# Gate and up projections of layer 0's second half: twelve slices as seven block products

## The chip, the cores and the metric

The kernel runs on one core of a Trainium2 chip. The metric is the device time of one execution in microseconds. Times in this document are medians of several runs, or come from one profiled execution where they are split into parts.

## The reference, cut to what matters

The model is a decoder trunk of two layers that computes one inference step for a prompt of 1024 tokens and a sample group of 8 tokens with the same weights. Each layer mixes the tokens (a gated recurrence in layer 0, stick-breaking attention in layer 1, in both beside attention into a memory) and then applies a SwiGLU feed-forward network. The change is in that network alone:

```python
def swiglu(h, w_gu, w_down):
    gate, up = jnp.split(h @ w_gu, 2, axis=-1)
    return (jax.nn.silu(gate) * up) @ w_down

h = h + rmsnorm(swiglu(rmsnorm(h, g[2]), w_gu[l], w_down[l]), g[3])
```

`h` has 1024 channels, `gate` and `up` 2816 each. Everything is in float32.

## The kernel before

**Groups and halves.** The tokens are worked on in two groups: group 0 has 512 prompt tokens, group 1 the other 512 and the 8 sample tokens, 520 columns in two halves of 260. Activations stand transposed: channels on the partitions, tokens along the columns. "The first half" of a layer is group 0's way through it, "the second half" group 1's.

**One projection.** To keep float32 accuracy every operand is split into a rounded part and the rest (`split_to` L280, `split_w` L250): ACT casts, DVE subtracts. A product takes three matmuls for each 128 x 128 block of weights: high by high, high by low, low by high. `proj` (L266) computes 128 output channels: it loads the weights in blocks of 512 x 128 over SP's queue into `wraw` (5 buffers), splits them into `wspl` (5 buffers), and accumulates eight blocks of 128 input channels in a tile of two PSUM banks, `mmp`, of which there are 2. For group 1 each matmul covers one half, 260 columns, so one projection is 8 x 3 x 2 = 48 matmuls.

**The feed-forward network.** The 2816 channels are 22 slices of 128, in five parts (`PARTS`, L613): 5, 5, 4, 4 and 4 slices. In `ffn.part` (L693) a slice is one projection for gate, SiLU by exponential, logarithm and exponential (`silu`, L284), one projection for up, the product of both, and its split into a tile of `mpool`. After the slices of a part comes the part's share of the down projection: eight products over the part's 4 or 5 slices, added into the result by `evac_raw` (L441).

**The seven products.** The last layer's second half (`ffn_w`, L615) already takes another way for its slices from the fifth on. `gate_up_w` (L524) regards gate and up of a slice as a product of 2 x 2 blocks: the weights' rows in two halves of 512, gate and up; the tokens in two halves of 260. By Winograd's form of Strassen's scheme it takes 7 block products of 4 x 3 = 12 matmuls (`product`, L546) where there were 8, 84 matmuls a slice in place of 96. It needs

- four sums of weight blocks, which `weight_sums` (L588) makes in DRAM: for each part eight DMAs of 1 MB (1.25 MB in the longer parts) on POOL's queue, four plain copies and four that accumulate. Each is let go by a mark: ACT copies one column of a tile just made (`after()`) into a small tile `tok`, POOL copies it on, and the DMA is issued behind that.
- four combinations of activations for each of four pairs of channel blocks, which `sums_w` (L326) makes on DVE and splits with ACT;
- four accumulators `pa` to `pd` (L557). They are chained: `pb` begins as the negated copy of `pa`, made by ACT after product 0, and `pc` as the negated copy of `pb` after product 2.

The products' order in a slice is: 0 into `pa`, 1 into `pd`, 2 into `pb`, 3 into `pa`, 4 into `pb`, 5 into `pc`, 6 into `pb`. In the last layer's second half the projections' PSUM tiles have been closed, and each accumulator has two banks of its own. Weight blocks are loaded there into `wraw` and, in every other case, into halves of tiles of `apool`.

**Order of work.** The program is recorded as generators that `weave` (L232) mixes by the weights written beside them; each `yield` is a step. A scheduler then orders the instructions of each engine. Around the change the text reads (L1462 to L1481, shortened):

```python
    f0 = ffn(0, 0, o0.x)
    weave((a1.core(), 22), (f0.part(0), 9))
    a1.open()
    weave((a1.sample(), 6), (a1.gate(), 4), (f0.part(1), 9))
    weave((chain(a1.merge(), a1.mem()), 12), (a1.mem_sample(), 20), (chain(f0.part(2), f0.part(3)), 16))
    drain(f0.part(4))
    ...
    f1 = ffn(1, 0, o1.x)
    ws = weight_sums(1, range(5), lambda: f1.now)
    weave((chain(b0.sb(), b0.mem()), 24), (chain(f1.part(0), f1.part(1)), 18), (islice(ws, 16), 17))
    weave((chain(f1.part(2), f1.part(3), f1.part(4)), 24), (ws, 24))
```

So `f0`, the first half's network of layer 0, runs beside the second group's mixer `a1`, which also reads the sample tokens' memory caches. `f1`, the second half's network of layer 0, runs parts 0 and 1 beside layer 1's mixer of the first group (`b0`) and parts 2 to 4 alone. Beside all of `f1`, layer 1's weight sums are made in DRAM.

Of the kernel before, what the change touches and what calls it, by code (L numbers as in the profile page):

```python
# [9 lines left out]
F32 = mybir.dt.float32  # L10
F32R = mybir.dt.float32r
# [13 lines left out]
def tile_decoder(  # L25
# [61 lines left out]
    def Q(i):  # L87
        return single[0].tile([P, 512], F32, tag=f"q{i}", name=nm("q"))
# [234 lines left out]
            out.append(x)  # L323
            yield

    def sums_w(xs, ops):  # L326

        n, h = NG[1], PW[1]  # L330
        for k in range(4):
            x0, x1 = xs[k], xs[k + 4]
            y = YT()
            if k % 2 == 0:
                z, u = YT(), YT()
            o = (k % 2) * h

            def full(x, c):
                t = B()
                nc.vector.tensor_add(t[:, :h], x[:, 0, c : c + h].bitcast(F32), x[:, 1, c : c + h].bitcast(F32))  # L340
                return t

            b11, b12, b21, b22 = full(x0, 0), full(x0, h), full(x1, 0), full(x1, h)
            for d, p, a, b in (
                (b11, u[:, :, o : o + h], b12, b11), (b12, y[:, :, h : 2 * h], b12, b22),
                (b22, y[:, :, :h], b22, b11), (b21, z[:, :, o : o + h], b21, b22),
            ):
                nc.vector.tensor_sub(d[:, :h], a[:, :h], b[:, :h])
# [7 lines left out]
    def YT():  # L356
        return xpool.tile([P, 2, NG[1]], F32R, tag="x0", name=nm("y"))

    def wo_tiles(g):
# [161 lines left out]
        split_to((mt[:, 0, :n], mt[:, 1, :n]), sg[:, :n])  # L521
        return mt, last

    def gate_up_w(l, f, ops, spl, raws):  # L524

        h, n = PW[1], NG[1]
        part, o = part_of(f)
# [26 lines left out]
                        start=(first and k == 0 and wi == 0), stop=(k == 3 and wi == 2), skip_group_check=True,  # L554
                    )

        pa, pb, pc, pd = (Q(i) for i in range(4))  # L557
        product(pa, 0, True)
        nc.scalar.activation(pb[:, :h], pa[:, :h], AF.Copy, scale=-1.0)
        product(pd, 1, True)  # L560
# [10 lines left out]
        product(pc, 5)  # L571
        nc.vector.tensor_sub(gt[:, :h], pc[:, :h], dt[:, h:n])
        product(pb, 6)
        nc.scalar.activation(sg[:, h:n], gt[:, :h], AF.Silu)
        nc.vector.tensor_mul(sg[:, :h], sg[:, :h], pb[:, :h])
# [3 lines left out]
        return mt  # L579

    sums = {}

# [32 lines left out]
    class ffn_w:  # L615


        def __init__(self, l, x, plain):
            self.g, self.l, self.x, self.ops, self.plain, self.n, self.r, self.pi = 1, l, x, [], plain, 0, 0, 0
            self.R = self.acc = None  # L620
            self.half = []
            self.sums = sums_w(x, self.ops)

        def spl(self):
            self.n += 1
# [13 lines left out]
        def part(self, pi):  # L639
# [4 lines left out]
            for j in range(nf):  # L644
                self.pi = pi
                if f0 + j < self.plain:
                    mt, ins = gate_up_q(l, f0 + j, self.x)
                    mids.append(mt)
                    with tc.issue_after(ins.ins):
                        for _ in range((1, 2, 1, 0)[j]):  # L650
                            next(self.sums, None)
                else:
                    mids.append(gate_up_w(l, f0 + j, self.ops, self.spl, self.raws))
                yield
            if pi == 0:
                self.R = R_one()
# [29 lines left out]
            yield from finish_rows(self)  # L686

    class ffn:
        def __init__(self, g, l, xt, rows=False):
            self.g, self.l, self.xt, self.rows = g, l, xt, rows  # L690
            self.R = self.acc = None

        def part(self, pi):  # L693
            g, l = self.g, self.l
# [2 lines left out]
            last = pi == len(PARTS) - 1  # L697
            mids = []
            for j in range(nf):
                pg = proj(g, w_gu[l], 0, ND, (f0 + j) * P, self.xt)  # L700
                sg = silu(None, pg, g)
                pu = proj(g, w_gu[l], 0, ND, DFF + (f0 + j) * P, self.xt)
                nc.vector.tensor_mul(sv(sg, g), sv(sg, g), pv(pu, g))  # L703
                mt = M(F32R)
                split_to((mt[:, 0, :n], mt[:, 1, :n]), sg[:, :n])
                mids.append(mt)
                self.now = sg[:, 0:1]
                yield
            if pi == 0:
                self.R = R_one()  # L710
            if last:
                self.acc = small([P, WID], tag="st", bufs=3)
            for m in range(ND):
                ps = proj(g, w_down[l], f0, nf, m * P, mids)
                evac_raw(g, self.R, ps, m, self.acc, pi == 0, last)
                self.now = self.R[m][:, 0:1]
                if last and self.rows:
                    nc.scalar.activation(
                        self.R[m][:, :n], self.R[m][:, :n], AF.Copy, scale=gcol(l, 3, m)
                    )  # L720
                    if m == 3:
                        first_half(self)
                if m % 2:
                    yield

        def finish(self, store):
# [733 lines left out]
    drain(o0.mm(a0.xo))  # L1460
    weave((o0.finish(), 17), (chain(a1.v(), a1.qm(A)), 8))
    f0 = ffn(0, 0, o0.x)  # L1462
    weave((a1.core(), 22), (f0.part(0), 9))
    a1.open()
    weave((a1.sample(), 6), (a1.gate(), 4), (f0.part(1), 9))
    weave((chain(a1.merge(), a1.mem()), 12), (a1.mem_sample(), 20), (chain(f0.part(2), f0.part(3)), 16))
    drain(f0.part(4))
    xk0, xb0 = [], []
    o1 = out_proj(1, 0, M)
# [67 lines left out]
```

## Time and profile before

| | us |
|---|---|
| median of 3 runs | 2504.36 (2503.7 to 2506.84) |
| the profiled execution | 2502.81 |
| its span, first to last instruction | 2501.1 |
| TensorE busy in the span | 2468.7 |
| DVE busy | 1571.7 |
| ACT busy | 1185.4 |

The time outside the span is 1.71 us. Layer 0's second half runs its parts 2 to 4 from about 1242 to 1451 us of the span. The views used below are: the page's first part; the timeline of an engine (start, length, engine, line, operation, what it writes and reads, count); a table of stretches with each engine's busy time, the clock that TensorE was granted and the share of the 16 DMA engines; groups of instructions by line (count, busy time and mean duration in ns, then the engine's idle time before them and what ended it); and the DMA view of a stretch, by queue (packets, MB, share) and by issuing line (count, size, median time from issue to landing). q0 is POOL's queue, q1 the one that SP feeds.

### The profile page before, as it was taken

What the parts mean: (1) busy time and instruction counts of PE and PEld (TensorE: products, weight loads), DVE (VectorE), ACT (ScalarE), POOL (GpSimd) and SP (SyncE); (2) the same over time, 40 slices, a digit from 0 to 9 for tenths busy, and PEclk for the clock granted to TensorE, in tenths of its full rate; (3) what the DMA queues carried; (4) which work ended last, traced back from release to release, by engine and by line L of the source; (5) the groups of instructions that cost most, each with busy time, mean ns of one, the idle gap of its engine ahead of it and who ended that gap; (6) DMA issues with size and microseconds to landing.
All of it is one profiled execution on the core that took longest, in us unless ns stands there. A gap on an engine that the chain in (4) does not pass through costs nothing. (4 is left out here: it accounts for less than half of the span.)

```text
span 2501.1 us, 40758 instructions
## 1 busy us (share of the span) xinstructions
PE 2468.7 (99%) x15565; PEld 2169.4 (87%) x15565; DVE 1571.7 (63%) x2756; ACT 1185.4 (47%) x2277; POOL 97.5 (4%) x139
## 2 busy tenths in 40 slices
PE   8999999999999999999999999999999999999998
PEld 6888888877877898999999989877787797999997
DVE  5766556754766585655544475777677648755665
ACT  5446544243434454555433454555444445564444
POOL 1000000000000000010111100022000000000000
PEclk9999999999999999999999999999999999999999
DMA  5352252134543447577678876544354234365542
GB/s 186 114 165 68 69 159 81 54 106 121 180 122 104 128 128 232 162 190 177 168 188 220 230 203 194 160 137 148 118 148 134 80 119 122 121 191 145 150 138 69
DMA packets 496109, 358.21 MB, mean 143 GB/s; under 512 B 19109, under 2 KB 443634, under 8 KB 495914
## 3 DMA queue, kind: packets, MB, share of 16 engines
q1 hardware_dynamic: 477354, 301.08, 40.2%
q0 software_dynamic: 18560, 54.53, 8.8%
q8 instruction: 122, 2.00, 0.3%
q14 instruction: 73, 0.60, 0.1%
HBM read 325.73 MB, written 75.94 MB: 161 GB/s over the span
## 5 line engine op out<-in xcount | busy, mean ns | idle before, releaser
L274 PE MATMUL mm<-x,ws 128*128 128x260 f32 (+1 forms) x7776 | 1344.1, 331 | 0.0
L274 PEld LDWEIGHTS mm<-x,ws 128*128 128x128 f32 x7776 | 1149.9, 188 | 152.9 <-issue 13.1
L260 ACT CAST ws<-w 128x512 fp32r<-128x512 f32 x712 | 420.2, 591 | 750.5 <-PE mm L274 615.1
L261 DVE TENSOR_TENSOR ws<-w,ws 128x512 fp32r<-128x512 f32 x712 | 463.4, 654 | 288.5 <-ACT ws L260 278.1
L274 PE MATMUL mm<-m,ws 128*128 128x512 f32 (+1 forms) x2112 | 400.2, 344 | 0.0
L274 PEld LDWEIGHTS mm<-m,ws 128*128 128x128 f32 x2112 | 324.3, 188 | 48.8 <-issue 2.2
L667 PE MATMUL q<-m,ws 128*128 128x260 f32 x1056 | 128.8, 283 | 0.0
L667 PEld LDWEIGHTS q<-m,ws 128*128 128x128 f32 x1056 | 127.2, 188 | 0.4 <-ACT hT L485 0.2
L543 DVE TENSOR_TENSOR ws<-w,ws 128x512 fp32r<-128x512 f32 x126 | 86.6, 692 | 60.3 <-ACT ws L542 57.6
L552 PE MATMUL q<-y,ws 128*128 128x260 f32 x864 | 112.9, 283 | 0.0
L542 ACT CAST ws<-w 128x512 fp32r<-128x512 f32 x126 | 78.0, 621 | 68.6 <-PE q L667 27.4
L552 PEld LDWEIGHTS q<-y,ws 128*128 128x128 f32 x864 | 107.6, 188 | 0.0
L447 DVE TENSOR_TENSOR r<-r,mm 128x512 f32<-128x512 f32 (+1 forms) x96 | 66.1, 689 | 65.7 <-PE mm L274 64.7
L291 DVE TENSOR_SCALAR t<-mm 128x512 f32<-128x512 f32 (+1 forms) x82 | 56.8, 693 | 78.7 <-PE mm L274 78.4
L703 DVE TENSOR_TENSOR t<-t,mm 128x512 f32<-128x512 f32 (+1 forms) x66 | 45.5, 690 | 75.7 <-PE mm L274 75.2
L295 DVE TENSOR_TENSOR t<-t,t 128x512 f32<-128x512 f32 (+1 forms) x66 | 45.8, 694 | 70.7 <-ACT t L294 70.7
L552 PE MATMUL q<-x,ws 128*128 128x260 f32 x648 | 86.3, 282 | 0.0
L552 PEld LDWEIGHTS q<-x,ws 128*128 128x128 f32 x648 | 81.3, 188 | 0.0
L314 DVE TENSOR_TENSOR st<-st,n 128x512 f32<-128x512 f32 (+1 forms) x98 | 67.3, 694 | 6.9 <-ACT n L313 5.2
L281 ACT CAST m<-t 128x512 fp32r<-128x512 f32 (+1 forms) x88 | 54.9, 624 | 18.4 <-DVE t L703 8.8
L282 DVE TENSOR_TENSOR m<-t,m 128x512 fp32r<-128x512 f32 (+1 forms) x88 | 61.0, 694 | 2.5 <-ACT m L281 1.4
L962 POOL DMA_INDIRECT c<-in_cache_sb_k,pidx x16 | 16.4, 1023 | 1172.9 <-ACT m L445 962.4
(339 smaller groups left out, 2565.6 us busy)
## 6 DMA issues: line engine op xcount, KB each, us to landing
w<-in_w_gu SPq DMA_DIRECT2D x334, 256.0 KB, 3.2
w<-in_w_down SPq DMA_DIRECT2D x160, 256.0 KB, 3.2
w<-in_w_in_a SPq DMA_DIRECT2D x80, 256.0 KB, 3.0
wsum<-in_w_gu POOLq DMA_DIRECT2D x18, 1024.0 KB, 9.0
w<-wsum SPq DMA_DIRECT2D x72, 256.0 KB, 3.7
w<-in_w_o SPq DMA_DIRECT2D x64, 256.0 KB, 2.8
wsum<-in_w_gu POOLq DMA_DIRECT2D x12, 1280.0 KB, 10.6
w<-in_w_mem_kv SPq DMA_DIRECT2D x32, 256.0 KB, 3.0
```

The lines of the kernel that those rows point to most:

```text
L260: nc.scalar.copy(ws[:, 0, :n, :], raw[:, :n, :])
L261: nc.vector.tensor_sub(ws[:, 1, :n, :], raw[:, :n, :], ws[:, 0, :n, :].bitcast(F32))
L274: nc.tensor.matmul(ps[:, a, : PW[g]], wt, xt[k][:, xi, o : o + PW[g]], start=(k == 0 and wi == 0), stop=(k == nk - 1 and wi == 2),)
L281: nc.scalar.copy(dst[0], src)
L282: nc.vector.tensor_sub(dst[1], src, dst[0].bitcast(F32))
L291: nc.vector.tensor_scalar(sv(x, g), pv(ps, g), -44.0, None, op0=ALU.max)
L314: nc.vector.tensor_add(acc[:, :n], acc[:, :n], t[:, :n])
L447: nc.vector.tensor_add(dst, dst, pv(ps, g))
L542: nc.scalar.copy(w[:, 0, :], src)
L543: nc.vector.tensor_sub(w[:, 1, :], src, w[:, 0, :].bitcast(F32))
L552: nc.tensor.matmul(ps[:, :h], w[:, wj, k * P : (k + 1) * P], x[:, xi, :], start=(first and k == 0 and wi == 0), stop=(k == 3 and wi == 2), ...
L667: nc.tensor.matmul(pp[a][:, :h], wt, mids[k][:, xi, a * h : (a + 1) * h], start=(k == 0 and wi == 0), stop=(k == nf - 1 and wi == 2),)
```

## The change

In layer 0's second half the slices 10 to 21, which are parts 2, 3 and 4, are computed by `gate_up_w`. `ffn` takes a parameter `prod`, the first slice that is done so; all other uses keep the old way.

- The four accumulators are the two PSUM tiles of the projections, `ta` (for `pa` and `pd`) and `tb` (for `pb` and `pc`); both buffers of `mmp` are in use by one slice.
- Weight blocks are loaded into `wraw` alone. Of every eight splits three go to `cpool` and five to `wspl`.
- The combinations of activations are made in the second half of part 1's down projection, one call of `sums_w` after every second of its eight products, in the eight buffers of `apool`.
- Layer 0's weight sums of parts 2 to 4, 24 DMAs of 1 MB on POOL's queue, are made beside `f0` in the first half.
- SiLU in these slices is ACT's own function, which needs another activation table; the table of logarithm and exponential is loaded again after the last slice.

```diff
-    def sums_w(xs, ops):
+    def sums_w(xs, ops, YT):
...
-    def gate_up_w(l, f, ops, spl, raws):
+    def gate_up_w(l, f, ops, spl, raws, quads):
...
-        pa, pb, pc, pd = (Q(i) for i in range(4))
+        pa, pb, pc, pd = quads()
...
     class ffn:
-        def __init__(self, g, l, xt, rows=False):
-            self.g, self.l, self.xt, self.rows = g, l, xt, rows
+        def __init__(self, g, l, xt, rows=False, prod=NF):
+            self.g, self.l, self.xt, self.rows, self.prod = g, l, xt, rows, prod
             self.R = self.acc = None
+            self.ops, self.n = [], 0
+            self.sums = sums_w(xt, self.ops, lambda: A(F32R))
+
+        def spl(self):
+            self.n += 1
+            if self.n % 8 in (1, 4, 6):
+                return cpool.tile([P, 2, 512], F32R, tag="c", name=nm("ws"))
+            return wspl.tile([P, 2, 512], F32R, tag="ws", name=nm("ws"))
+
+        def quads(self):
+            ta, tb = (mmp.tile([P, 2, 512], F32, tag="mm", name=nm("mm")) for _ in range(2))
+            return ta[:, 0, :], tb[:, 0, :], tb[:, 1, :], ta[:, 1, :]
...
             for j in range(nf):
+                if f0 + j >= self.prod:
+                    mt, gate = gate_up_w(
+                        l, f0 + j, self.ops, self.spl,
+                        lambda: wraw.tile([P, 4, P], F32, tag="w", name=nm("w")), self.quads,
+                    )
+                    mids.append(mt)
+                    self.now = mt[:, 0, 0:1].bitcast(F32)
+                    yield
+                    continue
                 pg = proj(g, w_gu[l], 0, ND, (f0 + j) * P, self.xt)
...
+            if last and self.prod < NF:
+                with tc.issue_after(gate.ins):
+                    nc.scalar.preload_act_table_set("natural_log_exp_and_others")
...
                 if m % 2:
+                    if f0 + nf == self.prod < NF:
+                        next(self.sums, None)
                     yield
...
     f0 = ffn(0, 0, o0.x)
-    weave((a1.core(), 22), (f0.part(0), 9))
+    ws = weight_sums(0, (2, 3, 4), lambda: f0.now)
+    weave((a1.core(), 22), (f0.part(0), 9), (islice(ws, 8), 8))
     a1.open()
-    weave((a1.sample(), 6), (a1.gate(), 4), (f0.part(1), 9))
-    weave((chain(a1.merge(), a1.mem()), 12), (a1.mem_sample(), 20), (chain(f0.part(2), f0.part(3)), 16))
+    weave((a1.sample(), 6), (a1.gate(), 4), (f0.part(1), 9), (islice(ws, 8), 8))
+    weave((chain(a1.merge(), a1.mem()), 12), (a1.mem_sample(), 20), (chain(f0.part(2), f0.part(3)), 16), (ws, 10))
...
-    f1 = ffn(1, 0, o1.x)
+    f1 = ffn(1, 0, o1.x, prod=10)
```

More of the change, by code (lines that the diff above doesn't have):

```diff
@@ L354, in sums_w, with Y0 @@
             yield
-    def YT():
+    def Y0():
         return xpool.tile([P, 2, NG[1]], F32R, tag="x0", name=nm("y"))
@@ L573, in gate_up_w @@
         product(pb, 6)
-        nc.scalar.activation(sg[:, h:n], gt[:, :h], AF.Silu)
+        last = nc.scalar.activation(sg[:, h:n], gt[:, :h], AF.Silu)
         nc.vector.tensor_mul(sg[:, :h], sg[:, :h], pb[:, :h])
@@ L578, in gate_up_w @@
         split_to((mt[:, 0, :n], mt[:, 1, :n]), sg[:, :n])
-        return mt
+        return mt, last
     sums = {}
@@ L621, in __init__ @@
             self.half = []
-            self.sums = sums_w(x, self.ops)
+            self.sums = sums_w(x, self.ops, Y0)
         def spl(self):
@@ L652, in part @@
                 else:
-                    mids.append(gate_up_w(l, f0 + j, self.ops, self.spl, self.raws))
+                    mids.append(gate_up_w(
+                        l, f0 + j, self.ops, self.spl, self.raws, lambda: [Q(i) for i in range(4)]
+                    )[0])
                 yield
```

## The prediction

> **What bounds the kernel now.** I read the cores and the page's first part, then TensorE's timeline through the stage that is changed and through the last layer's second half, which runs the same products already, then the table of stretches, the DMA view of the stage, and the operations at one slice boundary.
>
> ```profile
> core 0: 2501.1 us, clock 0.997
> PE 2468.7 (99%) x15565; PEld 2169.4 (87%) x15565; DVE 1571.7 (63%) x2756; ACT 1185.4 (47%) x2277; POOL 97.5 (4%) x139
> ```
>
> The clock is full. TensorE is the bound, with 2501.1 - 2468.7 = 32.4 us idle in all. Time can be won only by giving it less to do, and any wait that reaches it is lost in full.
>
> ```profile
> 1313.16 46.08 PE L274 MATMUL mm<-x,ws 128*128 128x260 f32 x384
> 1359.07 23.21 PE L274 MATMUL mm<-m,ws 128*128 128x260 f32 x192
> ...
> 2418.72 1.60 PE L552 MATMUL q<-x,ws 128*128 128x260 f32 x12
> ...
> 2457.63 1.61 PE L552 MATMUL q<-y,ws 128*128 128x260 f32 x12
> 2459.08 11.71 PE L667 MATMUL q<-m,ws 128*128 128x260 f32 x96
> ```
>
> These are rows of TensorE's timeline: start, length, line, operation, count. The first is the four gate and up slices of one part of layer 0's second half, from 1313.16 to 1359.07: 45.91 us for 4 x 96 matmuls. The second is the part's down projection. The others are the first and last product of four slices in the last layer's second half, which are already 7 block products of 12 matmuls: from 2418.72 to 2459.08, 40.36 us for 4 x 84. Both stages run without a hole, at 0.1196 and 0.1201 us a matmul.
>
> ```profile
> core 0: us, PE busy (x) PEld busy (x) DVE busy (x) ACT busy (x) POOL busy (x), PEclk, DMA share, GB/s
> 530.00:900.00 370.00, 370.00 (x1747) 290.89 (x1746) 229.98 (x360) 152.46 (x278) 0.00 (x0) 1.00 0.43 130
> 1202.00:1242.00 40.00, 39.93 (x289) 37.22 (x288) 20.42 (x44) 16.96 (x45) 3.40 (x5) 1.00 0.77 178
> 1242.00:1451.00 209.00, 208.88 (x1739) 208.38 (x1738) 105.24 (x156) 84.47 (x156) 32.97 (x49) 1.00 0.82 213
> 2418.70:2459.10 40.40, 40.40 (x339) 40.40 (x338) 25.33 (x46) 23.71 (x49) 0.00 (x0) 1.00 0.40 118
> ```
>
> The stretches are, in order: the first half's FFN of layer 0; the down projection just ahead of the changed slices; the three changed parts; the four slices of the last layer. The last column but one tells most: in the changed parts the DMA engines are already 82% busy, because layer 1's weight sums are made in DRAM there. In the last layer the same products run at 40%.
>
> **The products, part by part.** Three parts of four slices lose 4 x 12 matmuls each, 144 in all. By the two stages that is 45.91 - 40.36 = 5.55 us a part, **-16.6 us** for three, provided that TensorE stays as dense.
>
> ```profile
> L542 ACT CAST ws<-w 128x512 fp32r<-128x512 f32 x126 | 78.0, 621 | 68.6 <-PE q L667 27.4
> L543 DVE TENSOR_TENSOR ws<-w,ws 128x512 fp32r<-128x512 f32 x126 | 86.6, 692 | 60.3 <-ACT ws L542 57.6
> ```
>
> A slice splits 7 weight blocks instead of 4: three more casts of 0.62 us and three more subtractions of 0.69 us; its SiLU by three activations goes, and eight operations on 260 columns come. In the last layer the whole of it keeps DVE busy 25.33 of 40.4 us and ACT 23.71, so both engines have room, and I cost it at nothing as long as the order of work lets them run ahead. There are three places where it does not.
>
> **The accumulators.** In the last layer each of the four accumulators has two banks to alternate between. Here four accumulators take the whole of the projections' two tiles, once.
>
> ```profile
> 2300.61 1.61 PE L552 MATMUL q<-y,ws 128*128 128x260 f32 x12
> 2302.06 1.59 PE L552 MATMUL q<-x,ws 128*128 128x260 f32 x12
> 2302.42 0.42 DVE L575 TENSOR_TENSOR t<-t,q 128x260 f32<-128x260 f32 x1
> 2302.87 0.63 ACT L281 CAST m<-t 128x520 fp32r<-128x520 f32 x1
> 2303.70 0.37 ACT L559 ACTIVATE q<-q 128x260 f32<-128x260 f32 x1 [0.20 <-PE q L552]
> ```
>
> This is a slice boundary of the last layer. Product 6 ends when the next slice begins, at 2302.06. DVE reads its accumulator from 2302.42, ACT casts the slice's result from 2302.87, and ACT's negated copy into an accumulator of the next slice stands behind that cast. In the changed kernel the copy also has to wait for DVE's reading, since it writes the same tile; behind the cast it would start near 2303.45 and end near 2303.82, 1.8 us after product 6. The order of the built program puts only product 1, 12 matmuls or 1.44 us, between product 6 and product 2, which needs the copy (product 0 of the next slice is drawn ahead into the slice before). TensorE waits some 0.4 us at each of 3 x 3 boundaries inside the parts: **+3.6 us**; none if the copy slips ahead of the cast (then 1.4 us are enough), some 0.6 us more each if one more cast stands in the way, so 0 to 9.
>
> **The sums of the activations.** Four calls in the second half of the down projection ahead, 1202 to 1242. Each has 4 additions, 4 differences and 4 split subtractions on DVE and 4 casts on ACT, all on 260 columns.
>
> ```profile
> L570 DVE TENSOR_TENSOR t<-t,q x18: 418/418/426, 2175.1 to 2456.8; 128x260 f32<-128x260 f32 x18
> L568 ACT COPY t<-q x18: 370/370/373, 2173.9 to 2455.3; 128x260 f32<-128x260 f32 x18
> ```
>
> 48 x 0.418 = 20.1 us come to DVE, which is busy 20.42 of those 40, and 16 x 0.37 = 5.9 us to ACT at 16.96. With the first W blocks, which DVE must split in the same stretch (five at 0.69, 3.5 us), DVE has 44 us of work in 40. Queued behind it are the down projection's additions, which free the accumulators that TensorE needs next, and the softmax of the memory attention, for which TensorE's transposes wait in order. One result, some 5 us, can be late before TensorE feels it. Between nothing and the overrun with 0.5 us for each of 16 waits on a cast, 12 us: I take **+3 us**.
>
> **The weights.** 84 block loads take the place of 48, so 36 more.
>
> ```profile
> q0 software_dynamic: 8833, 23.56, 46.9%
> q1 hardware_dynamic: 38119, 20.78, 34.3%
> ...
> w<-in_w_gu SPq DMA_DIRECT2D x40, 256.0 KB, 6.1
> w<-in_w_down SPq DMA_DIRECT2D x24, 256.0 KB, 5.4
> ...
> q0 software_dynamic: 364, 0.75, 105.1%
> q1 hardware_dynamic: 21, 0.01, 1.3%
> ...
> q0 software_dynamic: 186, 0.76, 100.0%
> q1 hardware_dynamic: 24, 0.01, 2.0%
> ```
>
> The first four lines are the DMA view from 1242 to 1451: packets, MB and share of the engines for the weight sums (q0) and for everything that SP issues (q1), then loads with their time to land. The next pair is four microseconds from 1309.5, within an accumulating sum; the last pair two microseconds from 1319, within a plain copy. While a sum moves, almost no weight packet does, though a load is pending. So weights and sums share the engines one after the other. A sum has 1.05 MB: 5.6 us when it accumulates (0.75 MB in 4 us), 2.8 us when it copies (0.76 MB in 2 us). A weight block costs 34.3% of 209 us over 20.78 MB, 3.45 us a MB, so 0.90 us.
>
> A slice takes 7 x 0.90 = 6.3 us of weights plus one sum, in 10.1 us: with an accumulating one 11.9 (1.8 too much), with a copy 9.1 (1.0 to spare); each part has two of each. The down projection takes 8 x 0.90 + 2 x 5.6 + 2 x 2.8 = 24.0 in 23.2 us. A part is short by 2 x 1.8 - 2 x 1.0 + 0.8 = 2.4 us, three parts by 7. Against that stand five raw buffers and eight split ones, 13 blocks of 1.44 us, filled during a down projection, and layer 1's sums may finish late, since nobody reads them before the last layer. With everything covered it costs nothing. With no cover but the five raw buffers, a buffer's round is 6.1 us to land, 0.62, 0.69 and some 0.5 us in queues, 7.9 us, so 1.58 us a block instead of 1.44: 84 x 0.14 = 12 us. I take **+3 us**, nearer to the covered end because the deficit is a seventh of the cover in each part.
>
> [...]
>
> **The first half.** 24 more sums run between about 530 and 900, of 1.05 MB at 23.56 MB for 46.9% of 209 us, 4.2 us a MB: 105 us of DMA in 370, on top of a share of 0.43, so 0.71. Its weights are loaded at the old pace, and TensorE has not a hole in 370.00 us. 24 marks on ACT and POOL and two activation table changes lie on engines that are half idle. The second group's memory caches are loaded there too, and a sum ahead of one of those loads would delay it by 5.6 us: 0 to 6, I take **+0.5**. The prefetch of the page cache moves on POOL's queue behind the sums, to after the changed slices, and is not read before layer 1's second half: nothing.
>
> **Sum.** -16.6 + 3.6 + 3 + 3 + 0.5 = **-6.5 us**. The profiled execution took 2502.81 us for a span of 2501.1 us, 1.55 under the median of 2504.36, and would come to 2496.3; the median to **2498 us**.
>
> **Rivals.** *All of it arrives*: DVE's sums and the boundaries hide, the buffers cover the rest: 2504.4 - 16.6 = **2488 us**. For it: the last layer does the same without a hole. Against it: it has two banks for each accumulator, twice the raw buffers, and no sums on the DMA engines.
>
> *Nothing is left*: the costs take their middle to upper values, 9 us for the weights rather than 3 and 5 for the activations' sums: -16.6 + 3.6 + 5 + 9 + 0.5, **2506 us**, within what can't be told from no change. 0.2%, about 5 us, is what a measurement of this kernel can tell.
>
> *The weights come too late*, the slower case.
>
> ```profile
> w<-in_w_gu SPq DMA_DIRECT2D x8, 256.0 KB, 8.1
> ```
>
> This is the landing time in the down projection from 1290 to 1313, where four sums chain. If the doubled demand makes 8.1 us the rule in the slices, a raw buffer's round is 9.9 us, 1.98 us a block, 0.54 over what TensorE takes. The first 13 blocks of a part are covered, the other 45 of three parts are not: 45 x 0.54 = 24 us. With the other costs -16.6 + 3.6 + 3 + 24 + 0.5, **2519 us**. It eats the whole gain from 9.5 us on, that is 0.21 us a block, a round of 8.3 us, a landing of 6.5 us: little more than the 6.1 seen now. For it: the landing times of before, at half the demand. Against it: with five raw blocks on their way, landings of 5 to 8 us have cost TensorE nothing so far, and the engines' load is only a few per cent over 1.
>
> **How the numbers follow.** The forecast's neighbourhood (2491 to 2499) 0.37; all of it (2487 to 2491) 0.17; nothing left (2499 to 2509) 0.24; too late (over 2509) 0.22. So faster 0.54, same 0.24, slower 0.22. The range goes from the full gain, 2487, into the slow case as far as 2513, which leaves out about 0.15. The likeliest case's own range is 2491 to 2499.
>
> **What would show it.** Right: the four slices of a part near 41.5 us instead of 45.91, TensorE waiting for ACT's negated copy by 0.3 to 0.5 us nine times, DVE over 95% busy from 1202 to 1242, a DMA share near 1 in the changed parts. Wrong: idle time of TensorE before products that ends with the weights' subtraction, after casts that waited for a load; or idle time before 1000 us.

## The result and the profile after

The changed kernel takes **2572.15 us** (2569.8 to 2578.0, six runs) against 2505.43 (2503.67 to 2506.84, six runs) before: ratio **1.0271**, 95% interval 1.0259 to 1.0283. It is 66.7 us slower; forecast were 2498 us, 6.5 less, with a range of 2487 to 2513. The profiled execution's span grew by 69.0 us.

The cores' view of the kernel after, the page's first part, and its stretches: the first half, the down projection ahead, the three changed parts.

```profile
core 0: 2570.1 us, clock 0.987
```

```profile
PE 2481.3 (97%) x15421; PEld 2172.8 (85%) x15421; DVE 1598.5 (62%) x2852; ACT 1208.6 (47%) x2379; POOL 122.5 (5%) x187
```

```profile
core 0: us, PE busy (x) PEld busy (x) DVE busy (x) ACT busy (x) POOL busy (x), PEclk, DMA share, GB/s
530.00:900.00 370.00, 366.71 (x1711) 286.42 (x1711) 224.47 (x354) 150.56 (x289) 20.06 (x32) 1.00 0.63 174
1207.00:1247.00 40.00, 34.05 (x245) 31.43 (x243) 29.70 (x76) 19.31 (x54) 2.43 (x5) 0.97 0.71 158
1247.00:1512.00 265.00, 218.62 (x1589) 210.14 (x1590) 119.20 (x211) 99.44 (x217) 32.30 (x51) 0.91 0.78 205
```

There are fewer matmuls and TensorE is busy longer all the same. The changed parts take 265 us instead of 209. The removed matmuls did go: 1589 x 0.120 us would be 191 us. TensorE stands idle for 46 (265.0 - 218.6), and it is busy for 28 more than 191: the same matmuls take longer. The granted clock of 0.91 accounts for some 24 of these 28 (0.09 x 265). The stretch ahead lost 6 us, the first half 3.

Groups by line in the changed parts, after, and then the two groups before that answer to them (busy time and mean ns, then idle time ahead and what ended it):

```profile
L552 PE MATMUL mm<-a,ws 128*128 128x260 f32 x576 | 84.8, 304 | 24.0 <-ACT mm L559 19.6 <-DVE t L572 4.1
L274 PE MATMUL mm<-m,ws 128*128 128x260 f32 x561 | 77.9, 301 | 16.7 <-DVE r L447 16.7
L542 ACT CAST ws<-w 128x512 fp32r<-128x512 f32 x80 | 48.5, 618 | 91.9 <-DMA w<-wsum 38.6 <-PE mm L552 27.4 <-DMA w<-in_w_gu 14.6
```

```profile
L274 PE MATMUL mm<-m,ws 128*128 128x260 f32 x576 | 69.6, 282 | 0.0
L260 ACT CAST ws<-w 128x512 fp32r<-128x512 f32 x72 | 44.8, 622 | 115.7 <-PE mm L274 114.3 <-issue 1.3
```

The ACT rows tell most. Before, ACT waited before its weight casts for TensorE alone, to give back a split buffer: the weights were there. Now 53.2 us of its waits are for a load. TensorE waits mainly for two things: ACT's negated copy (L559, 19.6 us), and DVE's additions of the down projection (L447, 16.7 us here and 4.6 at a product). The second looks like a slow DVE, and it is not, as the timeline of all engines in the second changed part's down projection shows:

```profile
1401.11 13.26 PE L274 MATMUL mm<-m,ws 128*128 128x260 f32 x107
...
1403.50 1.02 POOL L606 DMA_DIRECT2D wsum<-in_w_gu  x1 [0.19 <-issue]
...
1405.97 0.37 SPq L537 DMA_DIRECT2D w<-in_w_gu  x1
...
1407.47 0.65 POOL L608 DMA_DIRECT2D wsum<-wsum  x1 [0.27 <-issue]
...
1417.60 0.62 ACT L542 CAST ws<-w 128x512 fp32r<-128x512 f32 x1 [10.76 <-DMA w<-in_w_gu]
1418.12 0.61 ACT L260 CAST ws<-w 128x512 fp32r<-128x512 f32 x1
1418.25 0.69 DVE L543 TENSOR_TENSOR ws<-w,ws 128x512 fp32r<-128x512 f32 x1 [8.89 <-ACT ws L542]
...
1419.46 0.69 DVE L447 TENSOR_TENSOR r<-r,mm 128x520 f32<-128x520 f32 x1
...
1420.29 5.11 PE L274 MATMUL mm<-m,ws 128*128 128x260 f32 x22 [5.92 <-DVE r L447]
```

A load for a slice of the next part is issued at 1405.97, between two sums, and its cast begins 11.6 us later. ACT stands 10.76 us at this cast, DVE 8.89 us at the subtraction behind it. What the program has next for each engine waits as well: the down projection's own casts (L260) and additions (L447), which do not need this load. Without the additions TensorE has no free accumulator.

### The profile page after: what moved, and what is told of

Its sections match the earlier page's. It is cut to its first block, busy times and chain, and to the rows that moved or that the text cites. A ratio compares the mean times of both kernels' runs of the same rounds, so it can differ in the third digit from the quotient of the medians.

```text
span 2570.1 us, 40844 instructions
## 1 busy us (share of the span) xinstructions
PE 2481.3 (97%) x15421; PEld 2172.8 (85%) x15421; DVE 1598.5 (62%) x2852; ACT 1208.6 (47%) x2379; POOL 122.5 (5%) x187
## 5 line engine op out<-in xcount | busy, mean ns | idle before, releaser
L274 PE MATMUL mm<-x,ws 128*128 128x512 f32 (+1 forms) x6624 | 1205.3, 339 | 1.1 <-DVE r L447 1.1
L274 PEld LDWEIGHTS mm<-x,ws 128*128 128x128 f32 x6624 | 1011.8, 188 | 154.2 <-issue 13.1
L260 ACT CAST ws<-w 128x512 fp32r<-128x512 f32 (+1 forms) x664 | 389.9, 589 | 634.5 <-PE mm L274 482.8
L261 DVE TENSOR_TENSOR ws<-w,ws 128x512 fp32r<-128x512 f32 (+1 forms) x664 | 429.1, 650 | 273.0 <-ACT ws L260 267.6
L274 PE MATMUL mm<-m,ws 128*128 128x512 f32 (+1 forms) x2112 | 411.7, 350 | 21.8 <-DVE r L447 21.8
L274 PEld LDWEIGHTS mm<-m,ws 128*128 128x128 f32 x2112 | 332.9, 193 | 73.0 <-ACT ws L542 16.6
L543 DVE TENSOR_TENSOR ws<-w,ws 128x512 fp32r<-128x512 f32 x210 | 144.1, 690 | 153.5 <-ACT ws L542 150.1
L542 ACT CAST ws<-w 128x512 fp32r<-128x512 f32 x210 | 128.8, 620 | 166.7 <-DMA w<-wsum 46.1
L552 PE MATMUL mm<-a,ws 128*128 128x260 f32 x576 | 84.8, 304 | 24.0 <-ACT mm L559 19.6
L552 PEld LDWEIGHTS mm<-a,ws 128*128 128x128 f32 x576 | 78.5, 206 | 28.7 <-ACT mm L559 22.3
L447 DVE TENSOR_TENSOR r<-r,mm 128x512 f32<-128x512 f32 (+1 forms) x96 | 65.8, 686 | 40.0 <-PE mm L274 38.9
L603 POOL COPY mk<-rr 128x1 f32<-128x1 f32 x64 | 21.7, 339 | 1372.9 <-ACT rr L602 1372.9
```

What stands on the lines that cost most here:

```text
L260: nc.scalar.copy(ws[:, 0, :n, :], raw[:, :n, :])
L261: nc.vector.tensor_sub(ws[:, 1, :n, :], raw[:, :n, :], ws[:, 0, :n, :].bitcast(F32))
L274: nc.tensor.matmul(ps[:, a, : PW[g]], wt, xt[k][:, xi, o : o + PW[g]], start=(k == 0 and wi == 0), stop=(k == nk - 1 and wi == 2),)
L447: nc.vector.tensor_add(dst, dst, pv(ps, g))
L542: nc.scalar.copy(w[:, 0, :], src)
L543: nc.vector.tensor_sub(w[:, 1, :], src, w[:, 0, :].bitcast(F32))
```

## The experiments

All times are medians; the kernel before took 2504.3 to 2505.6 us beside them. "Plain blocks" means that a weight block is read in place of a sum, so that the sum is missing from the result. The diffs show the lines that matter.

**Layer 1's sums beside the changed slices.**

```diff
-    ws = weight_sums(1, range(5), lambda: f1.now)
+    ws = weight_sums(1, range(2), lambda: f1.now)
```

> The changed kernel without layer 1's weight sums of parts 2 to 4, the 24 DMAs that run beside the changed slices; the last layer loads plain weight blocks in their place, so its loads stay as many and as large. Theory 'late weights': a weight block that lands late holds up ACT's casts, which are worked off in order, and behind them DVE's subtractions and evacuations. Then the 265 us of the changed stage (1247 to 1512) shrink to about 205, ACT's waits for loads there (53 us) nearly vanish, the granted clock returns to 1.0, and the total falls from 2572 to about 2500 to 2512. Rival 'the slices themselves': five raw buffers, single accumulators and the scheduler's order cost the time also without the sums: then the total stays above 2550.

Measured: 2527.41 us, ratio 1.0088 (1.0071 to 1.0105). 45 of the 67 us go; 22 stay, where at most 7 were expected. So neither theory holds alone.

> The kernel before without layer 1's weight sums of parts 2 to 4 (the last layer loads plain weight blocks in their place): the control. TensorE has no hole in that stage, so both theories expect no change, 2503 to 2506. If it falls by more, the sums cost TensorE something in the kernel before as well, and the run without them on the changed kernel has to be read against this one.

Measured: 2505.09, ratio 0.9998 (0.9989 to 1.0008). The same sums cost nothing beside the old slices.

> The changed kernel with layer 1's weight sums of parts 2 to 4 made later, beside layer 1's first half, instead of beside the changed slices. Theory 'late weights': like the run without these sums, if the sums hurt nobody in their new place, so 2500 to 2515; the new place has DMA engines 40 to 50% busy and plain slices that ask for a load each 2.9 us. Rival 'the slices themselves': above 2550.

```diff
     f0 = ffn(0, 1, o0.x)
+    ws = weight_sums(1, (2, 3, 4), lambda: f0.now)
...
-        (chain(f0.part(0), f0.part(1), f0.part(2), f0.part(3)), 34),
+        (chain(f0.part(0), f0.part(1), f0.part(2), f0.part(3)), 34), (ws, 24),
```

Measured: 2545.27, ratio 1.0162 (1.0145 to 1.0179), 18 us over e1: moved sums cost there too.

**Layer 0's sums in the first half.**

```diff
-    ws = weight_sums(0, (2, 3, 4), lambda: f0.now)
+    ws = iter(())
```

> The changed kernel without layer 0's weight sums beside the first half; the changed slices load plain weight blocks in their place. The first half lost about 5 us between 700 and 800 us. If that is the sums' doing, the total falls by 4 to 6 us, to about 2567, and the holes of TensorE between 700 and 800 us go; the changed stage stays as it is. If the first half were the main cause, the total would fall by tens of us. 'Late weights' and 'the slices themselves' both expect 2567.

Measured: 2566.3, ratio 1.0242 (1.0225 to 1.026): 5.9 us less than the changed kernel. The two intervals touch, so the size is uncertain; in the profiles the down projection ahead of the changed slices begins 4.5 us earlier (1200.1 against 1204.6).

**The accumulators.** What stayed in e1 is seen at a slice boundary of that kernel:

```profile
1340.04 1.70 PE L552 MATMUL mm<-a,ws 128*128 128x260 f32 x12
...
1341.80 0.42 DVE L575 TENSOR_TENSOR t<-t,mm 128x260 f32<-128x260 f32 x1
...
1342.35 0.62 ACT L281 CAST m<-t 128x520 fp32r<-128x520 f32 x1
...
1342.87 0.37 ACT L559 ACTIVATE mm<-mm 128x260 f32<-128x260 f32 x1
...
1343.29 3.15 PE L552 MATMUL mm<-a,ws 128*128 128x260 f32 x24 [1.55 <-ACT mm L559]
```

The first row is product 6, which ends at 1341.74. Behind it comes the chain as predicted: DVE's reading, the cast, the copy. But product 1 (the first half of the last row) stands behind the copy, not beside it. `pd`, into which it goes, shares the tile `ta` with `pa`, which the copy reads, and the wait is kept for the whole tile. So nothing covers the chain, some 1.5 us at each boundary. In the next kernels the four are apart:

```diff
             ta, tb = (mmp.tile([P, 2, 512], F32, tag="mm", name=nm("mm")) for _ in range(2))
-            return ta[:, 0, :], tb[:, 0, :], tb[:, 1, :], ta[:, 1, :]
+            return ta[:, 0, :], S(), S(), tb[:, 0, :]
```

> The changed kernel whole, but with the four accumulators of a slice kept apart: pa and pd, one bank of two different double tiles, and pb and pc in single banks of the pool that the softmax uses. So product 1 no longer shares a tile with what ACT's negated copy reads. Theory A (the loss has two causes that come on top of each other, late loads behind layer 1's sums and the accumulators' dependencies): the 20 us of waits at slice boundaries go where the weights are on time, but where the loads are late TensorE would wait anyway, so 5 to 20 us of the 67 come back: 2552 to 2567. Theory B (the loads alone set the stage's time): within 4 us of the changed kernel, 2568 to 2576. Theory C (the boundary's waits keep the engines out of step and are the root of the late splits): most of it comes back, under 2540.

> The same separate accumulators, and layer 1's weight sums of parts 2 to 4 left out as in e1_l1sums_out (plain blocks read in their place, which leaves those sums out of the result). Theory A (in e1 the stage's remaining loss was the shared tiles: 9 waits of 1.5 us for the negated copy, 3 of 0.5, and 0.2 to 0.3 us at two more places of a slice): 2527 less 16 to 22 us, 2505 to 2511. Theory B (the copy's wait hides a second one, of the splits of the next slice's weights, which then shows): 2518 or more. By A a slice inside a part takes 10.1 to 10.6 us instead of 12.4.

In e5 to e7 a part of the changed slices' result is wrong (last section); the instructions are the same. Measured: e5 2551.9, ratio 1.0194 (1.0177 to 1.0211), 20.2 us under the changed kernel; e6 **2504.31**, ratio 1.0003 (0.9993 to 1.0013), 23.1 under e1. Both come out as Theory A says, at or just under the lower end of its range. The edit also gives `pb` and `pc` more buffers than the two tiles have, so what separate tiles and what more buffers bring was not told apart. TensorE's timeline in e6, from the first product of a part to the part's down projection:

```profile
1323.60 1.61 PE L552 MATMUL mm<-x,ws 128*128 128x260 f32 x12
...
1364.01 23.20 PE L274 MATMUL mm<-m,ws 128*128 128x260 f32 x192
```

Four slices take 40.41 us, the last layer's 40.36. In parts 3 and 4 the products bring their full 5.5 us a part once loads and accumulators are out of the way. Yet e6 is only as fast as the kernel before, so 16.6 us are lost elsewhere: by the timelines some 4 in the first half, 8 in the down projection ahead, and 4 in the first of the three changed parts.

**Ahead of the changed slices.** e7 is e6 without the calls of `sums_w`; its `ops` hold plain rows:

```diff
-                    if f0 + nf == self.prod < NF:
-                        next(self.sums, None)
```

> As e6_own_accumulators_no_l1sums, and without the sums of the activations ahead of the changed slices: the products take plain rows of the activations as operands (the combinations are left out of the result). What is left against the kernel before is the removed matmuls, the 24 more weight sums of the first half, and the slices' own work. Theory A (DVE's queue is overrun in the 40 us ahead): 5 to 8 us under e6. Theory B (the waits there come from the first W blocks' splits, not from the sums): within 2 us of e6.

Measured: 2502.17, ratio 0.999 (0.998 to 0.9999), 2.1 us under e6: Theory B, at its edge. What stands there is a load again, in e6:

```profile
1227.94 1.01 POOL L611 DMA_DIRECT2D wsum<-in_w_gu  x1 [0.29 <-issue]
1231.16 0.71 SPq L537 DMA_DIRECT2D w<-in_w_gu  x1
1241.08 0.62 ACT L542 CAST ws<-w 128x512 fp32r<-128x512 f32 x1 [6.53 <-DMA w<-in_w_gu]
1243.46 0.62 PE L274 MATMUL mm<-m,ws 128*128 128x260 f32 x3 [3.03 <-DVE r L447]
```

In the kernel before a sum stood near this place, too (1223.70), and harmed nothing. Two attempts to clear it (e9 with `range(2)` in the second line and only 4 sums later). From e8 on, `pa` and `pd` of the first two slices stand in single banks of the softmax's pool, and the other accumulators as in e5:

```diff
+    pace = [f1]
-    ws = weight_sums(1, range(5), lambda: f1.now)
+    ws = weight_sums(1, range(5), lambda: pace[0].now)
-    weave(..., (islice(ws, 16), 17))
-    weave((chain(f1.part(2), f1.part(3), f1.part(4)), 24), (ws, 24))
+    weave(..., (islice(ws, 12), 13))
+    drain(f1.part(2), f1.part(3), f1.part(4))
...
     f0 = ffn(0, 1, o0.x)
+    pace[0] = f0
...
+        (chain(repeat(None, 22), islice(ws, 20)), 42),
...
-    weave((o1.finish(), 17), (f0.part(4), 8))
+    weave((o1.finish(), 17), (f0.part(4), 8), (ws, 8))
```

> The changed kernel with all its sums, in two things changed. The accumulators are apart: for the first two slices pa and pd in single banks and pb and pc in two double tiles, for the other ten as in e5_own_accumulators. And no sum of layer 1 is made from some 1190 us to the end of the changed slices: twelve are made ahead, at the old pace or a little faster, and the other 28 beside layer 1's half in the last part of the second group's attention and behind it, from some 1850 to 2170 us, when the DMA engines of before were 0.27 to 0.49 busy. Theory A (a sum costs only where a weight load that ACT's and DVE's queues wait for stands behind it): the removed matmuls bring 16.6 us, the first half's sums cost 5 to 6, the moved ones 0 to 5: 2493 to 2499. Theory B (sums cost wherever they are put, some 18 us as in e2_l1sums_moved): 2505 to 2512.

> As e8_sums_rearranged, without layer 1's sums of parts 2 to 4 (plain blocks are read in their place, which leaves those sums out of the result). Against e6_own_accumulators_no_l1sums only the last four sums of part 1 are moved, from 1190 to 1240 us to the second group. In e6 a weight load of the first changed slice was issued at 1231.16 us, behind the sum of 1227.94, and ACT's queue stood 6.53 us for it. Theory A (that one load is the price that looked like the activations' sums): 6 to 10 us under e6, 2494 to 2498. Theory B (DVE's overrun by the activations' sums is the price): within 2 us of e6, 2502 to 2506.

Here I erred: `weave` spread the twelve sums over the whole stretch instead of stopping early, and two still fell on 1210 and 1232 us. e9 took 2510.65, ratio 1.002 (1.0011 to 1.003), and had the same stall, 6.12 us of ACT's queue. e8 took 2525.87, ratio 1.0078 (1.0065 to 1.0092), above both its theories: 24 sums more in layer 1's half, some issued less than 1 us apart (1884.59 and 1885.37), cost it 15 us over e9. e11 is e9 with the weight 17 in place of 13.

> What e9_rearranged_no_l1sums was meant to be: there the twelve sums kept ahead were spread so that two still fell on 1210 and 1232 us. Here they go at the old pace, the last before some 1190 us, and the four others beside layer 1's half. No sums of layer 1's parts 2 to 4 (plain blocks in their place, left out of the result), accumulators apart. Theory A (the stall ahead of the changed slices is the one weight load behind a sum, which stops ACT's and DVE's queues): 7 to 11 us under e9_rearranged_no_l1sums, 2499 to 2503, or 2494 to 2498 if the boundaries of the first slices run as in e6_own_accumulators_no_l1sums. Theory B (DVE's overrun by the activations' sums): within 2 us of e9, 2508 to 2513.

Measured: 2502.79, ratio 0.9986 (0.9977 to 0.9996), 7.9 under e9: Theory A. Its stretch and its one long wait there, and then the same of e13 (below), which leaves the activations' sums out:

```profile
1200.00:1250.00 50.00, 45.58 (x330) 42.33 (x328) 43.00 (x106) 26.53 (x70) 0.00 (x0) 0.99 0.30 86
...
1250.10 1.09 PE L923 MATMUL s<-ident,b 128*128 128x128 f32 x4 [4.21 <-DVE b L916]
```

```profile
1200.00:1250.00 50.00, 46.86 (x340) 43.66 (x339) 27.35 (x57) 21.82 (x57) 3.59 (x6) 1.00 0.74 177
...
1249.53 0.30 PE L937 MATMUL s<-ident,b 128*128 128x128 f32 x1 [2.87 <-DVE b L930]
```

With no load late, DVE is 86% busy and TensorE waits 4.21 us once, for the softmax. That looks like the overrun of DVE that the prediction spoke of, but e13 waits 2.87 us at the same place with DVE 55% busy. So the activations' sums can answer for some 1.3 us of it. The rest is there without them: in both kernels the first product of these slices goes into a bank of the softmax's pool (`s`) and stands behind the softmax's transposes, where e6 had two products ahead of them. How the stages shifted, from the first and last matmuls of TensorE's timelines:

| | down projection ahead, us | first changed part's slices, us |
|---|---|---|
| before | 41.3 | 48.5 |
| changed | 49.3 | 52.0 |
| e6 | 49.6 | 46.5 |
| e7 | 49.6 | 45.4 |
| e9 | 49.4 | 51.5 |
| e11 | 41.5 | 53.0 |

The late load costs the down projection some 8 us. e11 wins them and loses 6.4 against e6 in the first part, so it is only 1.5 us faster. e9, with the same accumulators, loses 5 there, so they are the likely cause.

**Bandwidth, bursts or lead?** e10 keeps the sums of part 2:

```diff
-    ws = weight_sums(1, range(5), lambda: f1.now)
+    ws = weight_sums(1, range(3), lambda: f1.now)
...
-    weave((chain(f1.part(2), f1.part(3), f1.part(4)), 24), (ws, 24))
+    weave((chain(f1.part(2), f1.part(3), f1.part(4)), 24), (ws, 8))
```

> With the accumulators apart as in e8_sums_rearranged, and beside the changed slices only the eight sums of layer 1's part 2, spread evenly over the three parts, instead of 24 (those of parts 3 and 4 are left out of the result, plain blocks are read in their place). All 24 cost 47.6 us over none (2551.9 against 2504.3). The DMA engines' mean share in the stage was 0.56 without any sum; 24 sums add some 105 us of their time to 200, eight add 35, so 0.74. Theory A (bandwidth: the stage asks for more than the DMA engines have, and the shortage is the cost): with eight there is no shortage, 2504 to 2508. Theory B (each sum is a burst of 5.6 us that stops the loads, and costs wherever the raw buffers are not full, one by one): a third of it, 2516 to 2524.

Measured: 2526.96, ratio 1.009 (1.0074 to 1.0107). Theory B, and more than it asked: eight sums cost 22.6 us over e6, 2.8 each, at a DMA share of 0.64. Some 5 of the 22.6 may belong to the accumulators of the first two slices, which differ from e6's (e9 against e6 in the table). e12 cuts each sum in two (`cut` is 2 for them):

```diff
+                for r in range(0, 512, 512 // cut):
+                    dr, ar = (t[r : r + 512 // cut, :] for t in (d, a))
```

> e10_one_sum_in_three with each of its eight sums beside the changed slices cut into two of half the rows, each half with its own mark, so 16 transfers of 0.52 MB, evenly spread: the same bytes in bursts half as long (2.8 us when accumulating, 1.4 us when copying). The sums of parts 3 and 4 are left out of the result as there. Eight whole sums cost 22.6 us over none. Theory B1 (the cost is what a burst's length exceeds the raw buffers' cover of five blocks by): most of it goes, 2504 to 2512. Theory B2 (the cost goes by bytes, bursts or not): 2524 to 2530. Theory B3 (each transfer costs, by its start and its place in the queues): 2540 or more.

Measured: 2521.25, ratio 1.0064 (1.0045 to 1.0083): 5.7 us less. Neither B1 nor B2: bursts of half the length take back a quarter. So the lead was tested itself, by some ten raw blocks for five. The lead is what is loaded ahead of the cast that needs it:

```diff
+        def raws(self):
+            self.r += 1
+            if self.r % 2:
+                if not self.half:
+                    t = apool.tile([P, 2, 4, P], F32, tag="a", name=nm("w"))
+                    self.half = [t[:, 0], t[:, 1]]
+                return self.half.pop(0)
+            return wraw.tile([P, 4, P], F32, tag="w", name=nm("w"))
...
-                        lambda: wraw.tile([P, 4, P], F32, tag="w", name=nm("w")), self.quads,
+                        self.raws, self.quads,
```

> The control of e13_deep_eight_sums: the same, with the five raw buffers of the changed kernel (combinations of activations and the sums of parts 3 and 4 left out). All theories: e10's 22.6 us over e7's 2502, less 2 for the activations' sums being away, 2519 to 2526.

> As e10_one_sum_in_three (accumulators apart, eight sums beside the changed slices, those of parts 3 and 4 left out), but every other weight block of the changed slices is loaded into a half of a tile of apool, so that some ten raw blocks can be on their way instead of five. The eight buffers of apool come free because the combinations of activations are left out (plain rows of the activations are the operands, as in e7_no_activation_sums). Theory A (the loads have no lead: five raw buffers are all used by the slices themselves, so every burst arrives at TensorE): with ten the sums cost 0 to 5 us over e7's 2502: 2502 to 2507. Theory B (DMA time is short): as e15, 2518 to 2525.

> As e13_deep_eight_sums with all 24 sums of layer 1's parts 2 to 4 beside the changed slices (only the combinations of activations are left out). With five raw buffers they cost 47.6 us. The stage asks for some 112 + 105 us of the DMA engines in 192. Theory A (depth alone): 2502 to 2510. Theory B (DMA time alone): 2540 to 2550. Between: depth takes away what bursts do, and the missing 25 us of DMA time stays, less what the sums may finish late: 2515 to 2530.

Measured: e15 2528.56, ratio 1.0088 (1.0068 to 1.0107), 2.6 us above what was expected; e13 **2497.42**, ratio 0.9969 (0.9955 to 0.9983), 4.6 below its Theory A; e14 2516.43, ratio 1.0046 (1.003 to 1.0063), between its theories. ACT's waits between 1260 and 1450 us (total, times, longest), first in e15, then in e13:

```profile
ACT ws L542 <- DMA w<-wsum: 36.3, 13, 6.6
ACT ws L542 <- DMA w<-in_w_gu: 12.4, 7, 4.4
ACT ws L260 <- PE mm L274: 3.9, 2, 2.3
```

```profile
ACT ws L260 <- PE mm L274: 17.9, 12, 2.2
ACT ws L542 <- DMA w<-in_w_gu: 4.9, 2, 4.0
ACT ws L542 <- DMA w<-wsum: 1.8, 3, 0.8
```

The two kernels differ in one thing, the depth of the raw buffers. It is worth 31 us, and ACT waits for TensorE again. The down projection ahead mends itself with it: it takes 41.5 us in e13, 49.4 in e15. The 16 sums that e14 has more still cost 19 us at this depth. The stretch from 1250 to 1450 us of e14, and the waits in it:

```profile
1250.00:1450.00 200.00, 186.23 (x1505) 185.18 (x1505) 108.03 (x183) 94.02 (x199) 34.44 (x50) 0.96 0.89 227
...
ACT ws L542 <- DMA w<-in_w_gu: 13.5, 2, 11.0
...
PE mm L274 <- DVE r L447: 13.8, 3, 8.4
```

The DMA share is 0.89 on average, so DMA time may well be short here. But TensorE's 13.8 us of idle time are three waits in down projections, and one load was waited for 11 us: it is the chain seen before. Whether the average or a row of close sums makes the load late was not tested.

**Whole versions.** apool holds the activations' combinations, so the extra raw blocks go to cpool, and all splits to `wspl`:

```diff
-            if self.n % 8 in (1, 4, 6):
-                return cpool.tile([P, 2, 512], F32R, tag="c", name=nm("ws"))
...
-                    t = apool.tile([P, 2, 4, P], F32, tag="a", name=nm("w"))
+                    t = cpool.tile([P, 2, 4, P], F32, tag="c", name=nm("w"))
```

> The whole computation, the changed kernel with two edits: accumulators apart, and the deeper raw blocks in cpool as in e16_deep_rearranged; all sums where the changed kernel has them. By e14 2516.4 and 2 us for the activations' sums: theory A 2515 to 2521. Theory B (five splits are too few): near e5's 2552.

> The whole computation. Accumulators apart as in e8_sums_rearranged; every other raw block of the changed slices in a half of a tile of cpool (eight), the splits in wspl alone (five), so some ten raw blocks as in e13. Of layer 1's sums 16 ahead as in the changed kernel, eight beside the changed slices, 16 from some 1800 to 2170 us beside layer 1's half. By e13 2497.4, with 2 us for the activations' sums. Theory A (raw depth is all that matters, and 16 sums spread out later cost 0 to 5): 2499 to 2505. Theory B (five splits instead of eight take back what ten raw blocks give): 2515 or more.

Measured: e17 **2514.62**, ratio 1.0033 (1.002 to 1.0045), as Theory A says: two edits take back 57.5 of the 66.7 us. e16 2506.25, ratio 1.0007 (0.9997 to 1.0016), just above its Theory A. Two stretches of e16:

```profile
1250.00:1450.00 200.00, 199.31 (x1612) 196.95 (x1613) 120.49 (x201) 101.66 (x202) 18.93 (x24) 0.99 0.74 201
1600.00:2000.00 400.00, 389.73 (x1770) 298.01 (x1769) 280.84 (x436) 190.18 (x386) 47.28 (x48) 0.99 0.54 155
```

The changed slices run dense at last (199.31 of 200): their last down projection ends at 1443.6 us, 7.6 earlier than before. The gain is gone by the end, where the sums that had to go elsewhere run: TensorE was busy 396.2 of the 400 us from 1600 before, and 389.7 now. No whole version that I ran (e2, e8, e16, e17) beats the kernel before.

## Why the prediction was wrong

It failed in two steps, the weights and the accumulators; the first half's term was too small besides.

- **Products, -16.6: right**, where nothing else holds TensorE up. 40.41 us for four slices in e6 against 40.36.
- **Accumulators, +3.6: measured 20.2 (changed kernel to e5) to 23.1 (e1 to e6).** The chain behind product 6 took 1.5 us against 1.8. The step that failed is "only product 1 ... between", which was to cover 1.44 us of it: it writes the tile that the copy reads, so it waits as well. The views of the last layer could not show it, since there each accumulator has banks of its own; the code of `quads` did. Nine waits of some 1.5 us make 14; what else the shared tiles cost I did not take apart.
- **Activations' sums, +3: right in size.** 2.1 us by e7, 1.3 by the waits of e11 and e13.
- **Weights, +3: measured 47.6 beside the slices (e5 to e6) and 8 ahead of them (e9 to e11, and 49.3 us for 41.3 in the changed kernel's down projection).** I read the cover as 13 blocks that a down projection fills, and the deficit as 7 us over 209. What failed is the cover. The eight split buffers, it seems, are little lead if the loads behind them come through five raw ones, and the new slices use these five up even without a sum: in e6 ACT waits 27.7 us for loads in the stage, before the change not at all. That the raw depth is what was short is shown by e15 and e13: twice the depth, 31 us. With it 16 sums still cost 19 us (e13 to e14), against the 7 that I reckoned for 24; whether that is the average deficit stays open.
- **"The weights come too late" (2519)** had the mechanism, with 0.22. Its price, 24 us, was half of what was measured. It reckoned the delay in a raw buffer's round alone. A late load also holds up, in ACT's and DVE's queues, work that does not need it (the 10.76 and 8.89 us above), and after longer waits the matmuls ran at half the clock (granted 0.50 from 1420 to 1424 us, behind the wait of 5.92): by the stage's mean clock of 0.91 some 24 us, the estimate above.
- **"While a sum moves, almost no weight packet does"** held for a few microseconds only. In the changed kernel three loads are issued between 1404.8 and 1407.2 us, beside the two sums. The queues from 1405 to 1409 us, and then from 1409 to 1414:

```profile
q0 software_dynamic: 280, 0.57, 94.5%
q1 hardware_dynamic: 2, 0.00, 0.1%
...
q0 software_dynamic: 436, 1.25, 88.6%
q1 hardware_dynamic: 450, 0.23, 19.1%
```

For four microseconds, the start of the loads included, a sum alone moved, 280 packets against 2, as in the prediction's rows; then packets of loads and sums went by in about equal number, 450 and 436. So "almost no weight packet" was read from too short a stretch. The load of 1405.97, which also stood behind the one of 1404.8, took 11.6 us to its cast.

- **First half, +0.5: measured 5.9 (e3)**, at the upper end of its 0 to 6. "TensorE has not a hole" was true, and said nothing of how far ahead the loads ran.

The measured terms add up: -16.6 + 20.2 + 47.6 + 8 + 2.1 + 5.9 = 67.2 us against 66.7. They were measured in different kernels, and e11 shows that terms shift into one another, so the closeness is partly luck.

Of the signs that I named for "wrong", idle time before 1000 us came (3.2 us between 700 and 800). The other came in part: casts waited for loads, but TensorE's idle time ended with the negated copy and the additions, not with a weights' subtraction. Of those for "right" none came: the waits for the copy were 1.5 us and not 0.3 to 0.5, the DMA share was 0.78, and DVE was not over 95% busy from 1202 to 1242, since it stood behind a load, busy 29.7 of 40.

## What to carry to other kernels

Before doubling a stream's demand, look at what its consumer waits for: if the cast waits for TensorE (114.3 of its 115.7 us of waits in the kernel before) there is lead. How much can be estimated as raw blocks on their way times the time in which one is used up. Here that is 5 x 1.44 = 7.2 us, or 14.4 with ten, to be held against the longest time that a load took from issue to landing (12.2 us among the changed slices' blocks), not against the DMA engines' average share. One late load held ACT for 10.76 us and DVE for 8.89, with work behind it that did not need it, so price a late load by what is queued after its cast. And count dependencies by tile: two accumulators in one tile waited as one, 1.55 us at a boundary of e1.

## What the runs showed of the hardware

**Matmuls after a wait.** TensorE's rows from e12 (the first two) and e10 (the third), each a product of 12 matmuls:

```profile
1413.09 1.72 PE L552 MATMUL s<-a,ws 128*128 128x260 f32 x12 [0.72 <-ACT s L559]
1342.98 2.65 PE L552 MATMUL s<-a,ws 128*128 128x260 f32 x12 [2.37 <-ACT s L559]
```

```profile
1341.91 2.91 PE L552 MATMUL s<-a,ws 128*128 128x260 f32 x12 [3.18 <-ACT s L562]
```

A dense product takes 1.60 us. In the changed kernel, e5, e6, e8 to e12 and e15, after waits up to 1.74 us the next one took 1.68 to 1.73; after 1.78 us and more mostly 2.6 to 3.0. The granted clock (the last column but two) was 1.00 in e12 ahead of the wait of 2.37 us and 0.50 in the slow product behind it:

```profile
1338.00:1340.00 2.00, 2.00 (x19) 2.00 (x18) 0.31 (x1) 0.96 (x2) 0.00 (x0) 1.00 0.46 125
1344.00:1345.00 1.00, 1.00 (x7) 1.00 (x7) 0.79 (x2) 0.00 (x0) 0.00 (x0) 0.50 0.83 216
```

So the wait of 3.18 us cost over 4: 1.3 us more in the product behind it, and 0.4 in the next.

**Accumulators in single banks.** With `pb` and `pc` of all slices in single banks that the softmax had used (e5 to e7), a part of the result was wrong: in e5, which leaves no sum out, by a relative error of 0.28 in the worst output. With `pa` and `pd`, which begin with a matmul, in those banks for the first two slices, and `pb` and `pc`, which begin with ACT's copy, only from the third on (e8), nothing was. What was lost, and why, no run shows.
